# Hybrid decoder block on one core: a weight-sum buffer placed below the head products' pool, ScalarE casts pinned in program order, and an earlier second scan

## The chip, the cores and the metric

The kernel runs on one NeuronCore of one Trainium2 chip. The metric is the device time of one execution in microseconds (us). Five engines work side by side: TensorE (PE: matrix products, with its weight loads listed as PEld), VectorE (DVE), ScalarE (ACT), GpSimd (POOL) and SyncE (SP), which here issues the DMA transfers. Each executes its own instructions strictly in their order and waits, at the head of its queue, for whatever the next instruction needs.

## The reference

One decoder layer on a float32 `x` of 1024 tokens by 1024 channels:

```python
hn = rmsnorm(h, norm_mix); proj = hn @ w_in          # split into 12 parts
y_fox = fox_attention(fq, fk, fv, log_sigmoid(ff + bias))       # 8 heads of 128, causal, with forget bias
q, k, v = split(silu(causal_dwconv([gq, gk, gv], gdn_conv_w)))  # 4 taps
o = gated_delta_rule(l2norm(q), l2norm(k), v, g, beta)          # 8 heads, chunks of 64
y_gdn = rmsnorm(o, gdn_norm) * silu(gz)
h = h + (sigmoid(gate_fox) * (y_fox @ w_branch_fox)
         + sigmoid(gate_gdn) * (y_gdn @ w_branch_gdn)) @ w_out
u = causal_dwconv(rmsnorm(h, norm_ffn) @ w_up)                  # 3 taps
h = h + (silu(u_gate) * u_val) @ w_down
return rmsnorm(h, norm_final)
```

The delta rule is computed in chunks of 64: each needs the inverse of a 64 by 64 unit lower triangular matrix, and then a state of 128 by 128 per head is carried from chunk to chunk.

## The kernel before, in words

**Number format.** A float32 operand is cut into a rounded part (cast on ACT, L106) and the rest (a subtraction on POOL or DVE, L107), and each product is the sum of three: high by high, high by low, low by high. In the profile the pairs are `oh`/`ol` for weights, `yh`/`yl` for activations, `qh`/`ql` and `kh`/`kl` for attention, `vh`/`vl` for its values, `ph`/`pl` for the probabilities. The helper is `split`; `operand` makes an `oh`/`ol` pair, `wsplit` loads a weight tile `wr` and makes two.

**Who sets the order.** PE executes in the order of the code, which is written as generators that are stepped against each other (`take` steps one, `finish` drains it). On DVE, ACT, POOL and SP a scheduler chooses the order of ready work, except where the code pins it: `keep_in_program_order(x)` keeps pinned instructions of one engine in the order of the code, and `issue_after(x)` puts what is issued in its block behind `x` on `x`'s engine. Neither adds a wait on data.

**The stages** in order, with the time each takes in the trace, are in the table below. Those that the change touches:

- *Projection* (`project`): 32 jobs of 84 matmuls (L156, Strassen products of two weight chunks each), operands made three products ahead. Steps taken between matmuls carry other work. First come the delta-rule heads (pool `gin`), in parallel with `prepare_merge`, which adds up branch weights in 16 rounds: a DMA load into a buffer `msum` (L1012, one buffer, inside `gin`), four DVE operations (L993 to L996), a DMA store to `ms` (L1017). When the heads are done, `finish(sums)` drains what is left of those rounds, `gin` is closed, `factors` makes per-token factors (`brk`, and `brk2`, a product with `rk`, L861), and `inverse` starts: it loads `invz` (L940), copies `brk2` twice into `invb2` (L943), lets PE transpose it (L947, L949) and then walks 114 steps of two DVE operations each (L972, L974). Its 135 steps are spread so that they end 420 matmuls before the projection's end. Then `prepare_lead` (first operands of the feed-forward stage) and `fox_first`: loads of the first attention head, `fox_query` and `fox_key` (the casts of `qh` and `kh`), and the first logits (`probs`, L1116 to L1118 on PE).
- *Mix*: the attention of 8 heads (`fox`: per head eight row blocks `probs`, then two halves of `attend`: transposes L1153, products L1144) in 205 steps. Between them, two delta-rule scans are stepped (`stream(0)` for even heads, `stream(1)` for odd): `prep` (loads, POOL scalings of `svt` and `skt` L1241, small products), `scan` (PE L1267, L1272, L1278 to L1281, DVE `sr` and `ss`, ACT `su`, `so`, `sjk`), `columns` (POOL `srs`, `so` L1308; PE transposes L1313; `yge` L1317 on ACT for the last two heads; `ygd` stored). `fox_values` (casts of `vh` on ACT L1072, `vl` on POOL L1073) stands behind row block 5. After the attention both streams are drained.
- *Merge* (`merge`): seven Strassen products per branch (PE L1522), n = 0 to 6, each of four blocks k and 48 matmuls; each block's operands are split on ACT and DVE. After n = 0 of the first branch the columns of the last head are drained (its two `yge`).
- *Output product* (`mix_out`): PE L1514 with `oh`/`ol` of `w_out` and `yh`/`yl` of the merged rows.

Of the kernel before, what the change touches and what calls it, by code (L numbers as in the profile page):

```python
# [17 lines left out]
P = 128  # L18
# [4 lines left out]
H = 8  # L23
# [64 lines left out]
class Block:  # L88
# [14 lines left out]
    def split(self, hi, lo, src, lo_eng=None):  # L103

        nc = self.nc
        nc.scalar.copy(hi, src)  # L106
        (lo_eng or nc.vector).tensor_tensor(lo, src, hi.bitcast(F32), ALU.subtract)  # L107

# [608 lines left out]
    def project(self, blk, fox_pool):  # L717
# [3 lines left out]
        def spill(name, n=H):  # L721
# [10 lines left out]
        rk, self.rq, self.brk, self.brk2, self.kbn = (  # L732
            cp.tile([P, H, NB], F32, name=n) for n in ("rk", "rq", "brk", "brk2", "kbn"))
        gs = ExitStack()
# [122 lines left out]
        def factors():  # L857
# [3 lines left out]
            v.tensor_tensor(self.brk2, self.brk, rk, ALU.mult)  # L861
            v.scalar_tensor_tensor(self.kbn, self.brk2, -1.0, self.egc, op0=ALU.mult, op1=ALU.mult)
# [12 lines left out]
        sums = self.prepare_merge(pool)  # L875
        heads, wait, inv, prep, fox, left = 0, 24, None, None, None, len(jobs) * 84
        with ExitStack() as ix:
            for i, _ in enumerate(self.strassen(jobs, blk, pace=3)):
# [16 lines left out]
                elif inv is None:  # L895
# [3 lines left out]
                    finish(sums)  # L899
# [27 lines left out]
    def inverse(self, ip):  # L927
# [5 lines left out]
        b2 = ip.tile([P, 2, H * NB], F32, name="invb2")  # L933
# [8 lines left out]
        for s in range(2):  # L942
            nc.vector.tensor_copy(b2[:, s], self.brk2.rearrange("p h n -> p (h n)"))  # L943
# [3 lines left out]
        nc.tensor.transpose(ps[:, 0:P], b2.rearrange("p s n -> p (s n)"), self.ident)  # L947
        ps2 = self.small()
        nc.tensor.matmul(ps2[0:Q, 0:Q], self.ident[:, Q:P], b2[:, 0], start=True, stop=True)  # L949
# [70 lines left out]
    def prepare_lead(self, pool):  # L1020
# [5 lines left out]
        def load(src):  # L1026
            t = pool.tile([P, 1024], F32, tag="raw", bufs=4, name="raw")
# [30 lines left out]
    def fox_query(self):  # L1058

        for sl in (slice(0, 512), slice(512, 1024)):  # L1060
            self.split(self.qh[:, sl], self.ql[:, sl], self.ql[:, sl].bitcast(F32), self.nc.gpsimd)

    def fox_key(self):
        for sl in (slice(0, 512), slice(512, 1024)):
            self.split(self.kh[:, sl], self.kl[:, sl], self.kl[:, sl].bitcast(F32), self.nc.gpsimd)
# [881 lines left out]
```

## Time and profile before

| | |
|---|---|
| runs | 2019.66, 2024.9, 2028.93 us; median 2024.9 |
| profiled execution | 2022.93 us, of which the profile's span is 2021.2 us |
| granted TensorE clock, mean of the span | 0.988 |
| busy in the span: ACT, POOL | 1068.1 us (53%), 948.2 us (47%) |

By stage, from a table of windows (us):

| stage | stretch | PE busy | DVE busy | granted clock |
|---|---|---|---|---|
| norm and first operands | 0 to 125 | 108.2 | 85.6 | 1.00 |
| projection, with the heads | 125 to 480 | 336.1 of 355 | 272.1 | 0.98 |
| projection, with the inverse | 480 to 738 | 248.9 of 258 | 237.2 | 0.99 |
| projection, end | 738 to 830 | 90.7 of 92 | 46.9 | 1.00 |
| mix | 830 to 1094 | 242.8 of 264 | 199.1 | 0.97 |
| merge | 1094 to 1260 | 158.0 of 166 | 137.5 | 0.99 |
| output product | 1260 to 1390 | 123.7 of 130 | 88.0 | 0.99 |
| feed-forward, up | 1390 to 1800 | 404.5 of 410 | 302.7 | 1.00 |
| feed-forward, down | 1800 to 2021 | 212.0 of 221 | 126.8 | 0.99 |

"Busy" is the time in which an engine executes something; the rest of a stretch is idle. In a row of the timeline the columns are start, duration, engine, line, operation, output and inputs with their shapes; the bracket, where there is one, is the idle time of that engine just before it and what ended it. "Granted clock" is the TensorE clock that was granted, as a share of full speed; matmuls at 0.50 take twice as long, and count as busy.

### The profile page before, as it was taken

The numbers are of one execution on the slowest core, as the hardware profiler recorded it, in microseconds if no ns is written. First come the engines' busy times: TensorE is split into PE (matmuls) and PEld (weight loads), VectorE is DVE, ScalarE is ACT, GpSimd is POOL, SyncE is SP. The second block draws the span as 40 slices with busy tenths as digits, with TensorE's granted clock in tenths as the row PEclk, the third lists the DMA queues.
The fourth block names the chain that finished last, engine by engine and source line by source line (L and its number), as shares of the span: only waits on it lengthen the run. The fifth ranks groups of instructions, "written<-read, shape, count | busy, mean of one in ns | idle before, by whom it ended". The sixth has DMA issues, their size and how long they took to land. (4 is left out here: it accounts for less than half of the span.)

```text
span 2021.2 us, 29138 instructions
## 1 busy us (share of the span) xinstructions
PE 1924.9 (95%) x9628; PEld 1603.2 (79%) x9628; DVE 1495.9 (74%) x2546; ACT 1068.1 (53%) x2383; POOL 948.2 (47%) x792
## 2 busy tenths in 40 slices
PE   6999999997999899998998999999999999999998
PEld 6988887786878688788987787777788888877886
DVE  7839888864999975477777798577966767777535
ACT  5436777752333355466666444466655555553234
POOL 4735656563545556446563123134666566530012
PEclk9999999998999999899999999999999999999999
DMA  5235555564323277675754853665434343368654
GB/s 193 65 103 165 172 196 177 183 208 162 120 95 109 100 229 265 215 229 200 229 186 160 273 172 109 200 209 174 146 131 136 114 146 126 111 233 330 220 189 162
DMA packets 191608, 350.89 MB, mean 174 GB/s; under 512 B 50784, under 2 KB 79712, under 8 KB 191456
## 3 DMA queue, kind: packets, MB, share of 16 engines
q1 hardware_dynamic: 191312, 348.50, 51.5%
q8 instruction: 76, 1.25, 0.3%
q14 instruction: 76, 0.62, 0.1%
q10 hardware_dynamic: 144, 0.52, 0.1%
HBM read 232.76 MB, written 116.20 MB: 173 GB/s over the span
## 5 line engine op out<-in xcount | busy, mean ns | idle before, releaser
L107 POOL TENSOR_TENSOR ol<-ws,oh 128x512 fp32r<-128x512 f32 x212 | 290.3, 1372 | 232.0 <-ACT oh L106 227.1
L107 POOL TENSOR_TENSOR ol<-wr,oh 128x512 fp32r<-128x512 f32 x165 | 229.0, 1390 | 287.2 <-ACT oh L106 237.6
L106 ACT CAST oh<-ws 128x512 fp32r<-128x512 f32 x212 | 131.0, 618 | 187.3 <-PE mm L156 185.0
L202 DVE TENSOR_TENSOR ws<-wr 128x512 f32<-128x512 f32 x106 | 101.2, 955 | 122.4 <-DMA wr<-in_w_up_dram 65.3
L106 ACT CAST oh<-wr 128x512 fp32r<-128x512 f32 x204 | 123.4, 615 | 120.0 <-PE mm L156 85.5
L382 DVE SCALAR_TENSOR_TENSOR cv<-c,fw,cv 128x512 f32<-128x512 f32 (+2 forms) x176 | 127.5, 748 | 10.9 <-ACT cv L377 9.1
L382 DVE SCALAR_TENSOR_TENSOR cv<-c,cw,cv 128x511 f32<-128x511 f32 (+2 forms) x144 | 105.9, 748 | 8.4 <-ACT cv L377 6.5
L972 DVE TENSOR_TENSOR invt<-invz 128x399 f32<-128x399 f32 (+50 forms) x114 | 96.7, 863 | 0.3
L258 ACT COPY x<-mm 128x512 f32<-128x512 f32 x158 | 92.0, 582 | 5.6 <-PE mm L156 4.5
L156 PE MATMUL mm<-b22h,oh 128*128 128x512 f32 x216 | 85.6, 396 | 6.0 <-ACT x L258 6.0
L156 PE MATMUL mm<-bt1h,oh 128*128 128x512 f32 x216 | 85.3, 395 | 5.9 <-ACT x L258 5.8
L156 PE MATMUL mm<-bt4h,oh 128*128 128x512 f32 x216 | 85.9, 398 | 5.2 <-DVE c L305 5.2
L107 DVE TENSOR_TENSOR ol<-wd,oh 128x512 fp32r<-128x512 f32 x66 | 46.3, 705 | 58.6 <-ACT oh L106 58.6
L156 PE MATMUL mm<-bt4l,oh 128*128 128x512 f32 x216 | 86.9, 402 | 0.0
L156 PE MATMUL mm<-bt2h,oh 128*128 128x512 f32 x216 | 85.3, 395 | 1.3 <-ACT x L258 1.3
L156 PE MATMUL mm<-b21l,oh 128*128 128x512 f32 x216 | 86.2, 399 | 0.0
L156 PE MATMUL mm<-bt2l,oh 128*128 128x512 f32 x216 | 85.8, 397 | 0.3 <-DVE bt2l L107 0.3
L156 PE MATMUL mm<-b22l,oh 128*128 128x512 f32 x216 | 86.0, 398 | 0.0
L156 PE MATMUL mm<-b11h,oh 128*128 128x512 f32 x216 | 84.9, 393 | 1.0 <-ACT oh L106 1.0
L156 PE MATMUL mm<-b11h,ol 128*128 128x512 f32 x216 | 84.8, 393 | 0.6 <-POOL ol L107 0.6
L156 PE MATMUL mm<-bt4h,ol 128*128 128x512 f32 x216 | 85.2, 395 | 0.0
L156 PE MATMUL mm<-b11l,oh 128*128 128x512 f32 x216 | 85.2, 394 | 0.0
(407 smaller groups left out, 6360.8 us busy)
## 6 DMA issues: line engine op xcount, KB each, us to landing
wr<-in_w_up_dram SPq DMA_DIRECT2D x43, 512.0 KB, 3.7
wr<-in_w_gdn_dram SPq DMA_DIRECT2D x24, 512.0 KB, 3.8
wr<-in_w_out_dram SPq DMA_DIRECT2D x24, 512.0 KB, 4.3
s<-hy SPq DMA_DIRECT2D x44, 256.0 KB, 2.8
s<-z SPq DMA_DIRECT2D x44, 256.0 KB, 3.5
wd<-in_w_down_dram SPq DMA_DIRECT2D x44, 256.0 KB, 5.9
b22h<-s SPq DMA_DIRECT2D x44, 256.0 KB, 2.9
b22l<-s SPq DMA_DIRECT2D x44, 256.0 KB, 3.3
```

What stands on the lines that cost most here:

```text
L106: nc.scalar.copy(hi, src)
L107: (lo_eng or nc.vector).tensor_tensor(lo, src, hi.bitcast(F32), ALU.subtract)
L156: self.nc.tensor.matmul(ps, lhs[:, sl], rhs[:, k, :], start=(first and k == 0 and i == 0), stop=(k == 3 and i == 2), skip_group_check=True)
L202: v.tensor_tensor(t, x, y, op)
L258: nc.scalar.copy(t, x)
L382: nc.vector.scalar_tensor_tensor(t[:, lo:], c[:, 512 * j + lo - s:512 * (j + 1) - s], w[:, n - 1 - s:n - s], t[:, lo:], op0=ALU.mult, op1= ...
L972: nc.vector.tensor_tensor(tv, z[:, m:n, 0:n].to_broadcast([P, r, n]), z[:, m, c0:c1].unsqueeze(2).to_broadcast([P, r, n]), ALU.mult))
```

## The change

Line numbers below are those of before unless a row is of the changed kernel.

1. `prepare_merge` gets a pool of its own (`msum`), opened below `gin`, so its rounds need not be drained before `gin` closes: `finish(sums)` moves behind the inverse. `factors` writes `brk2` twice side by side, and PE transposes it directly; the buffer `invb2` and its copies are gone. The step `i % 84 in (24, 64, 80)` that advances the rounds stays.
2. The inverse is spread to end 360 instead of 420 matmuls before the end of the projection; `prepare_lead` has three `raw` buffers instead of four.
3. The casts of `qh` and `kh` (new helper `fox_parts`) are pinned in program order, and `fox_values` comes behind row block 4 instead of 5.
4. The scans: `prep` of head 1 starts at attention step 9 instead of 12, the second stream at 21 instead of 26; stream 0 takes the three steps of its last `columns` inside the stream, so the merge no longer drains them.
5. In the merge, the splits of n = 1 of the first branch stand behind the last `yge`. In the output product, the splits of a weight tile stand behind the `yh` cast before it.

```diff
@@ factors
-            v.tensor_tensor(self.brk2, self.brk, rk, ALU.mult)
-            v.scalar_tensor_tensor(self.kbn, self.brk2, -1.0, self.egc, op0=ALU.mult, op1=ALU.mult)
+            for s in range(2):
+                v.tensor_tensor(self.brk2[:, s], self.brk, rk, ALU.mult)
+            v.scalar_tensor_tensor(self.kbn, self.brk2[:, 0], -1.0, self.egc, op0=ALU.mult, op1=ALU.mult)
@@ project
-        gs = ExitStack()
+        gs, ws = ExitStack(), ExitStack()
+        sums = self.prepare_merge(ws.enter_context(tc.tile_pool(name="msum", bufs=1, reuse_waits="tile")))
         pool = gs.enter_context(tc.tile_pool(name="gin", bufs=1, reuse_waits="tile"))
...
-        sums = self.prepare_merge(pool)
...
-                    finish(sums)
                     gs.close()
                     factors()
...
-                    if (begin - left) * INVERSE_STEPS >= (begin - 420) * steps:
+                    if (begin - left) * INVERSE_STEPS >= (begin - 360) * steps:
                         steps += 1
                         if not take(inv, 1):
                             ix.close()
+                            finish(sums)
...
                     if left % 20 == 0 and not take(prep, 1):
                         ix.close()
+                        ws.close()
                         fox = self.fox_first(fox_pool())
@@ inverse
-        for s in range(2):
-            nc.vector.tensor_copy(b2[:, s], self.brk2.rearrange("p h n -> p (h n)"))
...
-        nc.tensor.transpose(ps[:, 0:P], b2.rearrange("p s n -> p (s n)"), self.ident)
+        nc.tensor.transpose(ps[:, 0:P], self.brk2.rearrange("p s h n -> p (s h n)"), self.ident)
@@ prepare_lead
-            t = pool.tile([P, 1024], F32, tag="raw", bufs=4, name="raw")
+            t = pool.tile([P, 1024], F32, tag="raw", bufs=3, name="raw")
@@ attention
+    def fox_parts(self, hi, lo):
         for sl in (slice(0, 512), slice(512, 1024)):
-            self.split(self.qh[:, sl], self.ql[:, sl], self.ql[:, sl].bitcast(F32), self.nc.gpsimd)
+            raw = lo[:, sl].bitcast(F32)
+
+            self.tc.keep_in_program_order(self.nc.scalar.copy(hi[:, sl], raw))
+            self.nc.gpsimd.tensor_tensor(lo[:, sl], raw, hi[:, sl].bitcast(F32), ALU.subtract)
...
-                if t == 5:
+                if t == 4:
                     self.fox_values()
@@ columns
-                        nc.scalar.activation(y, ps, AF.Copy, scale=self.gn[:, 0:1])
+                        self.evicted = nc.scalar.activation(y, ps, AF.Copy, scale=self.gn[:, 0:1]).ins
@@ mix
+                for _ in range(0 if s else 3):
+                    take(prev, 1)
+                    yield
                 self.last.append(prev)
...
-                if i in (0, 12):
+                if i in (0, 9):
                     preps[i > 0] = prep(int(i > 0))
-                if i in (0, 5, 7):
+                if i in (0, 6, 8):
                     take(preps[0], 1)
-                elif i in (12, 20, 23):
+                elif i in (9, 16, 19):
                     take(preps[1], 1)
-                if i >= 26:
+                if i >= 21:
...
-            for c in self.last:
-                take(c, 1)
+            take(self.last[1], 1)
@@ merge
-            if br == 0:
-                finish(self.last[0])
...
+                    elif br == 0 and n == 1:
+
+                        with self.tc.issue_after(self.evicted):
+                            w, y = self.merge_split(get(wn, k), get(yn, k), v)
@@ mix_out
+                    with self.tc.issue_after(cast) if cast else nullcontext():
+                        w = self.wsplit(a["w_out"][k],
+                                        nc.gpsimd if t0 == 6 and k % 2 == 0 or t0 == 3 and k < 2 else nc.vector)
...
-                            self.split(yh[:, sl], yl[:, sl], src[k][:, zl])
+                            cast = self.split(yh[:, sl], yl[:, sl], src[k][:, zl])
```

What this moves on three engines. First DVE, where `factors` ends and the inverse begins; before:

```order
L995 TENSOR_TENSOR msum<-msum 128x256
L996 TENSOR_TENSOR msum<-msum 128x256
L993 TENSOR_TENSOR msum<-msum 128x256
L994 TENSOR_TENSOR msum<-msum 128x256
L995 TENSOR_TENSOR msum<-msum 128x256
L996 TENSOR_TENSOR msum<-msum 128x256
L943 COPY invb_5134<-brk_1590 128x64 x2
L953 TENSOR_SCALAR invb<-ms 64x64 x2
L950 COPY brh<-ms 64x64
L289 TENSOR_TENSOR c_5175<-mm,x_5090 128x512
```

The same place on DVE with the change:

```order
L864 TENSOR_TENSOR brk_1591<-brk,rk 128x64 x2
L865 SCALAR_TENSOR_TENSOR kbn<-brk_1591,egc 128x64
L866 TENSOR_SCALAR brk<-brk 128x64
L306 TENSOR_TENSOR c_5070<-mm,x_5068 128x512
L993 TENSOR_TENSOR msum<-msum 128x256
L994 TENSOR_TENSOR msum<-msum 128x256
L995 TENSOR_TENSOR msum<-msum 128x256
L996 TENSOR_TENSOR msum<-msum 128x256
L321 TENSOR_TENSOR c_5070<-mm,x_5011 128x512
L203 TENSOR_TENSOR ws<-wr 128x512
```

The tile that PE transposes was the last thing behind the three rounds of sums that follow `factors` (L943; the rows show one and a half of them); now it is written by the second row of `factors` (L864), ahead of all three. One round stays in this place, and L953, which reads the transposed tile, comes six rows behind it; the other two rounds move between the first operations of the inverse, L960.

Second ACT, before the first attention head, where the projection's operands (`oh`), copies of its products (`x`), activations (`c`) and the first exponential (`p`) run; before:

```order
L106 CAST qh<-ql 128x512 x2
L106 CAST oh<-ws 128x512
L760 ACTIVATE c_7917<-c_7917 128x512
L106 CAST kh<-kl 128x512 x2
L106 CAST oh<-wr 128x512
L760 ACTIVATE c_7984<-c_7984 128x512
L106 CAST oh<-ws 128x512
L258 COPY x_8025<-mm 128x512
L106 CAST oh<-wr 128x512 x2
L258 COPY x_8068<-mm 128x512
```

The same stretch of ACT with the change, from the activation `c_7919` (`c_7917` above) on:

```order
L762 ACTIVATE c_7919<-c_7919 128x512
L106 CAST oh<-wr 128x512
L762 ACTIVATE c_7986<-c_7986 128x512
L106 CAST oh<-ws 128x512
L259 COPY x_8027<-mm 128x512
L106 CAST oh<-wr 128x512
L1069 CAST qh<-ql 128x512 x2
L106 CAST oh<-wr 128x512
L259 COPY x_8070<-mm 128x512
L1069 CAST kh<-kl 128x512 x2
```

The casts of `kh` stood ahead of four `oh` casts and two copies of products; now they stand behind all of these, one `oh` cast ahead of the first exponential.

Third POOL in the mix, at the second head's values, where the first scan's `columns` (`srs`, `so`) and the preparation of the next scan (`svt`, `skt`) run too; before:

```order
L1241 TENSOR_TENSOR svt<-svt,brk 128x512 x2
L1306 TENSOR_TENSOR srs<-srs,rq 128x8
L1308 TENSOR_TENSOR so<-so,srs 128x512 x2
L1241 TENSOR_TENSOR skt<-skt,dkl 128x512 x2
L1073 TENSOR_TENSOR vl<-vl,vh 128x512 x2
```

The same place on POOL with the change:

```order
L1246 TENSOR_TENSOR svt<-svt,brk 128x512 x2
L1311 TENSOR_TENSOR srs<-srs,rq 128x8
L1078 TENSOR_TENSOR vl<-vl,vh 128x512 x2
L1313 TENSOR_TENSOR so<-so,srs 128x512 x2
L1246 TENSOR_TENSOR skt<-skt,dkl 128x512 x2
```

`vl` moves ahead of two pairs of POOL operations. On ACT, the merge's rows change as the diff says: with the change all eight casts of n = 1 stand behind the four copies `p` of n = 0 and the two `yge`, where before five of the eight stood ahead of the two `yge`. In the output product the first tile's four `oh` casts stood ahead of all `yh`; with the change the first `yh` stands behind two of them.

More of the change, by code (lines that the diff above doesn't have):

```diff
@@ L1 @@
-from contextlib import ExitStack
+from contextlib import ExitStack, nullcontext
 import numpy as np
@@ L105, in split @@
         nc = self.nc
-        nc.scalar.copy(hi, src)
+        cast = nc.scalar.copy(hi, src)
         (lo_eng or nc.vector).tensor_tensor(lo, src, hi.bitcast(F32), ALU.subtract)
+        return cast.ins
     def operand(self, src, lo_eng=None):
@@ L729, in project @@
         self.gt_d = spill("gtd", 2 * KD)
-        rk, self.rq, self.brk, self.brk2, self.kbn = (
-            cp.tile([P, H, NB], F32, name=n) for n in ("rk", "rq", "brk", "brk2", "kbn"))
-        gs = ExitStack()
+        rk, self.rq, self.brk, self.kbn = (cp.tile([P, H, NB], F32, name=n) for n in ("rk", "rq", "brk", "kbn"))
+        self.brk2 = cp.tile([P, 2, H, NB], F32, name="brk2")
+        gs, ws = ExitStack(), ExitStack()
+        sums = self.prepare_merge(ws.enter_context(tc.tile_pool(name="msum", bufs=1, reuse_waits="tile")))
         pool = gs.enter_context(tc.tile_pool(name="gin", bufs=1, reuse_waits="tile"))
@@ L932, in inverse @@
         br = ip.tile([P, Q], F32, name="invb")
-        b2 = ip.tile([P, 2, H * NB], F32, name="invb2")
         self.y_d = dr.tile([Q, P, Q], F32, name="yd")
@@ L946, in inverse @@
         ps = self.small()
-        nc.tensor.transpose(ps[:, 0:P], b2.rearrange("p s n -> p (s n)"), self.ident)
+        nc.tensor.transpose(ps[:, 0:P], self.brk2.rearrange("p s h n -> p (s h n)"), self.ident)
         ps2 = self.small()
-        nc.tensor.matmul(ps2[0:Q, 0:Q], self.ident[:, Q:P], b2[:, 0], start=True, stop=True)
+        nc.tensor.matmul(ps2[0:Q, 0:Q], self.ident[:, Q:P], self.brk2[:, 0].rearrange("p h n -> p (h n)"), start=True, stop=True)
         nc.vector.tensor_copy(self.brh.rearrange("p h n -> p (h n)"), ps2[0:Q, 0:Q])
@@ L1537, in products @@
             def products(t0, n, ps):
+                cast = None
                 for k in range(KD):
-                    w = self.wsplit(a["w_out"][k], nc.gpsimd if t0 == 6 and k % 2 == 0 or t0 == 3 and k < 2 else nc.vector)
+                    with self.tc.issue_after(cast) if cast else nullcontext():
+                        w = self.wsplit(a["w_out"][k],
+                                        nc.gpsimd if t0 == 6 and k % 2 == 0 or t0 == 3 and k < 2 else nc.vector)
                     yh = pool.tile([P, 3 * P], F32R, tag="yh", bufs=2, name="yh")
```

6 lines of the change are left out of this document (3 added, 3 removed).

## The prediction

> **What bounds the kernel now.** I read the page's first part, then the chain, then PE's timeline for every row with idle time before it, and only then the engine that each such row waited for.
>
> ```profile
> span 2021.2 us, 29138 instructions
> PE 1924.9 (95%) x9628; PEld 1603.2 (79%) x9628; DVE 1495.9 (74%) x2546; ACT 1068.1 (53%) x2383; POOL 948.2 (47%) x792
> ...
> PE 31%; DVE 2%; ACT 1%; POOL 1%; DMA 1%; issue 1%; SPq 0%; POOLq 0%; ACTq 0%; DVEq 0%
> ```
>
> PE works 1924.9 of 2021.2 us, and the chain names it most. The change leaves its products as they are, so there are two things to win: the 96.3 us in which PE idles, and the time in which it works at a lowered clock behind a longer idle. Everything below is counted in these two.
>
> **A. The start of the inverse.** The longest single idle of PE, and what stands before it on DVE and SP (SPq):
>
> ```profile
> 460.96 0.43 DVE L993 TENSOR_TENSOR msum<-msum 128x256 f32<-128x256 f32 x1 [2.87 <-DMA msum<-in_w_branch_dram]
> ...
> 470.32 0.42 DVE L993 TENSOR_TENSOR msum<-msum 128x256 f32<-128x256 f32 x1 [7.08 <-DMA msum<-in_w_branch_dram]
> ...
> 472.04 0.29 DVE L943 COPY invb<-brk 128x64 f32<-128x64 f32 x2
> ```
>
> ```profile
> 446.82 0.23 DVE L861 TENSOR_TENSOR brk<-brk,rk 128x64 f32<-128x64 f32 x1
> ```
>
> ```profile
> 472.47 0.45 PE L947 MATMUL ms<-ident,invb 128*128 128x128 f32 x1 [12.62 <-DVE invb L943]
> ```
>
> ```profile
> 466.07 1.25 SPq L1012 DMA_DIRECT2D msum<-in_w_branch_dram  x2
> ...
> 475.08 2.27 SPq L940 DMA_DIRECT2D invz<-zd  x4
> ```
>
> ```profile
> 472.50:478.00 5.50, 5.50 (x14) 4.20 (x15) 1.35 (x4) 0.00 (x0) 1.29 (x1) 0.51 0.59 175
> ```
>
> The copies that PE's transpose needs stand in DVE's queue behind two rounds that wait 2.87 and 7.08 us for their one buffer: its load (466.07) can only follow the round before. The product that is copied is ready at 447.05. With the change the tile is written there, and the first round behind it no longer holds anything of PE's. PE would want it at 459.85 (472.47 less 12.62), so nothing takes this wait's place: **-12.6 us**. The window behind it (its columns: PE, PE loads, DVE, ACT, POOL busy; granted clock; DMA share; GB/s) shows the clock at 0.51 for 5.5 us, of which half is lost: -2.7 us. The load of `invz`, the last of the SP rows, is issued at the start of the inverse and moves with it. **A is -15.3 us**; the wait alone, -12.6, is its lower bound.
>
> **B. The inverse.** What bounds it, in 25 us windows, and PE's waits in the stage (total, times, longest):
>
> ```profile
> 575.00:600.00 25.00, 22.69 (x92) 18.05 (x92) 24.86 (x40) 7.66 (x14) 9.49 (x8) 0.93 0.29 105
> ...
> 625.00:650.00 25.00, 24.92 (x110) 20.27 (x109) 24.86 (x38) 11.36 (x21) 12.74 (x9) 1.00 0.32 106
> 650.00:675.00 25.00, 20.17 (x83) 15.89 (x82) 24.83 (x36) 7.89 (x15) 10.36 (x7) 0.95 0.24 85
> ```
>
> ```profile
> PE mm L156 <- DVE c L305: 5.2, 2, 2.9
> PE mm L156 <- ACT x L258: 3.8, 2, 1.9
> ```
>
> ```profile
> L972 DVE TENSOR_TENSOR invt<-invz 128x399 f32<-128x399 f32 (+50 forms) x114 | 96.7, 863 | 0.3
> ```
>
> DVE is full here (24.83 to 24.86 of 25), the 114 operations of L972 alone take 96.7 us, and what PE needs of DVE is late by what does not fit: 5.2 + 3.8 = 9.0 us of idle, and by the clocks 0.93 and 0.95 another 1.75 + 1.25 = 3.0 us. The change gives the inverse 60 more matmuls, 60 x 0.227 = 13.6 us (110 of them start in the 24.92 us of the middle window), and puts two rounds of sums into it:
>
> ```profile
> 125.00:480.00 355.00, 45.99 (x64) 0.98 0.56 180
> ```
>
> The row holds DVE's operations on `msum` alone: 64 in 45.99 us make a round of four cost 2.9 us, so 5.7 us are added. Net relief for DVE is 13.6 - 5.7 = 7.9 us against some 12 us of loss. It is not all won: the middle window shows DVE as full with PE hardly idle, so the lateness depends on which steps fall together, not on the mean. Bounds: 0 (they fall together again) and -12. I take **-5 us**, a little under the middle. `prepare_lead` starts 13.6 us later by this; its work lies beside products whose operands are made three products ahead, which cover it, so it is taken at 0; without that cover PE would meet its DVE work as it meets B's.
>
> The bare price of a round is 4 x 0.43 = 1.7 us (by the rows at 460.96 and 470.32). The Trainium skill, "GPSIMD Engine Reference", section 1, says that GpSimd's SBUF interfaces are shared with VectorE and contended by its operations with two SBUF inputs, which these are. In the three windows POOL is busy 9.5 to 12.7 of 25 us, so by that rule the mean of 2.9 holds; by the bare 1.7 the relief would be 2.4 us larger.
>
> **C. The first head's casts.** ACT, POOL and PE before:
>
> ```profile
> 794.26 1.13 ACT L106 CAST kh<-kl 128x512 fp32r<-128x512 f32 x2
> ...
> 804.24 0.58 ACT L258 COPY x<-mm 128x512 f32<-128x512 f32 x1
> ```
>
> ```profile
> 799.46 1.29 POOL L107 TENSOR_TENSOR kl<-kl,kh 128x512 fp32r<-128x512 f32 x1
> ```
>
> ```profile
> 805.61 0.28 PE L1117 MATMUL ms<-kl,qh 128*128 128x256 f32 x1
> ```
>
> Today `kl` is done 4.9 us ahead of L1117. Pinned, the `kh` cast stands behind that copy `x`, which ends at 804.82; half a cast later (0.57) POOL can start, and needs up to 1.3 us for the operand in front and 1.29 us for the first half of `kl`: 806.7 to 808.0, against 805.61. PE's clock may dip behind such a wait, for 0 to 1.75 us by B's first window. Lateness 1.1 to 2.4 and half of that dip make 2.6; **C is +3 us** with the next `oh` cast's `ol` queued behind `kl` on POOL, bounds 0 (the scheduler's queue runs ahead of PE) and +5: a new wait where there is none, L1117 behind POOL's `kl`.
>
> **D. The mix.** PE's waits in 837 to 1095 and the largest of them:
>
> ```profile
> PE us L1267 <- ACT so L1289: 4.0, 3, 1.6
> PE ya L1144 <- POOL vl L1073: 3.9, 2, 3.7
> PE ms L1153 <- DVE p L1132: 2.8, 2, 1.9
> PE ya L1144 <- ACT pf L1161: 1.9, 2, 1.1
> ```
>
> ```profile
> 906.26 2.04 POOL L1241 TENSOR_TENSOR svt<-svt,brk 128x512 f32<-128x512 f32 x2 [2.22 <-DMA svt<-vtd]
> ...
> 908.86 2.04 POOL L1308 TENSOR_TENSOR so<-so,srs 128x512 f32<-128x512 f32 x2
> ...
> 913.24 2.94 POOL L1073 TENSOR_TENSOR vl<-vl,vh 128x512 fp32r<-128x512 f32 x2
> ```
>
> ```profile
> 900.00:925.00 25.00, 20.98 (x153) 18.66 (x152) 18.07 (x61) 16.73 (x51) 18.96 (x20) 0.93 0.64 216
> ```
>
> `vl` moves ahead of `so` and `skt`, so it starts 4.4 us earlier (913.24 - 908.86), at 908.9: the 3.7 us wait goes, with the dip of clock (0.07 x 25 = 1.75 us). It still stands behind `svt` and its 2.22 us of DMA, so nothing more is won there. The `kh` and `qh` casts leave the row blocks for the second half of attention, which should shorten the waits for `so` and `pf`, ACT rows both; but four more casts of ACT then stand among that half's `ph`. And the second scan starts five steps sooner and shares ACT and DVE for longer, with less slack at its end. I count -5.4 for `vl` and -0.6 for the rest: **D is -6 us**, bounds -14 (all four rows and the clock) and +5 (as much again as the new neighbours' waits would cost, by the sum of the third and fourth row).
>
> **E. End of the mix, start of the merge.** The first block after n = 0, and what lies up to n = 2:
>
> ```profile
> 1106.11 1.04 PE L1313 MATMUL ms<-ident,so 128*128 128x128 f32 x8
> ...
> 1111.58 0.50 PE L1522 MATMUL b<-yh,oh 128*128 128x512 f32 x1 [3.04 <-ACT yge L1317]
> ...
> 1119.93 0.50 PE L1522 MATMUL b<-yl,oh 128*128 128x512 f32 x1 [1.20 <-DVE yl L107]
> ...
> 1127.63 0.50 PE L1522 MATMUL a<-yh,ol 128*128 128x512 f32 x1 [2.40 <-DVE ol L107]
> ```
>
> ```profile
> 1110.83 0.69 ACT L1317 ACTIVATE yge<-ms,gn 128x512 f32<-128x512 f32 x1
> ```
>
> ```profile
> 1112.00:1114.00 2.00, 2.00 (x7) 1.27 (x6) 2.00 (x3) 1.03 (x2) 2.00 (x2) 0.70 1.06 384
> ```
>
> n = 1 and its waits take 1127.63 - 1106.11 = 21.5 us, of which 48 x 0.227 = 10.9 are its products, 0.9 the transposes, 6.6 the waits. With the casts behind both `yge` the evictions come first (0.69 us each, the first when half of the transposes are done), then the first pair of casts (1.13, by C's row): ACT is done 0.5 + 1.4 + 1.1 = 3.0 us after 1106.11, and with 0.2 of handing over PE starts 2.3 us after the transposes, where it started at once. If the later waits go, that is 0.9 + 2.3 + 10.9 = 14.1 us, with a dip of clock up to 15.8: a gain of 5.7 to 7.4. Against it: DVE is full (2.00 of 2.00 in the window) and DMA too (1.06), so what DVE must make of n = 1 and of n = 2's sums may be the limit. Bounds -7.4 and +4 (the waits stay, 2.3 and its dip of clock are added). I take **-3.5 us**, with 0.6 of it for the scan's tail, whose steps move into the attention.
>
> **F. Output product.**
>
> ```profile
> PE mm L1514 <- DVE yl L107: 1.8, 1, 1.8
> PE mm L1514 <- ACT yh L106: 0.9, 1, 0.9
> ```
>
> The first `yh` cast moves ahead of two `oh` casts (1.13 us for two casts of that size, by C's row), so the 0.9 goes, and a third of the 1.8 behind it: **-1.5 us**, bounds -2.7 and +2 (the operand casts now pinned behind a `yh` come late once, as the 1.8 did).
>
> **The sum**: -15.3 - 5 + 3 - 6 - 3.5 - 1.5 = -28.3. The profiled execution took 2022.93 us (span 2021.2 and 1.7 around it), so 1994.6; the median of the runs is 2.0 us above it: **1996.6 us**.
>
> On the dips: the windows that hold B's two waits of DVE's `c`, none over 2.9 us, read 0.93 and 0.95. The Trainium skill, "TensorE: Matmul & The Clock Gate", section "Why this matters for your kernels", asks that no idle gap exceed some 3 us. By that rule C's wait would cost no clock, and the sum would be 0.9 us better; these windows speak against it.
>
> **The rivals.** (1) *Only the first wait goes* (chance 0.18): DVE stays full in the inverse, and POOL and ACT in the mix pass the wait on to another row. For it: B's windows and E's, where DVE has no gap; against it the 7.9 us of room in B, and `vl`, which plainly moves. Time: -15.3 + 3 = -12.3, so 2012.6. (2) *The inverse pays it back* (0.06): the rounds come later, each waiting for its buffer on DVE as the 2.87 and 7.08 did, now among operations that PE needs. Two such waits return 9.95 us of the 12.3 that rival 1 leaves: 2022.5, no change. Against it: the rounds' loads are issued 16 matmuls or more ahead by the code. (3) *Slower: handing over from head to head* (0.04). The pinned `kh` cast comes at the fourth step of the second half, so POOL's `kl` may not be there at the next head's L1117.
>
> ```profile
> 921.35 0.66 PE L1153 MATMUL ms<-ident,p 128*128 128x128 f32 x4 [0.18 <-DVE yge L1320]
> ...
> 931.53 0.28 PE L1117 MATMUL ms<-kl,qh 128*128 128x256 f32 x1
> ```
>
> PE takes 10.2 us from that step to L1117; cast and both subtractions need 1.13 + 2.6 = 3.7, so 6.5 us of cover remain, and only `svt` with its DMA (4.3) is seen to stand between. Beyond 6.5 us of lateness each us costs seven heads one us each, so it needs over 5.5 us more in each to eat 28.3 and 10 on top: 2036. (4) *All is won* (0.06): B and D at their better ends, 15 us more than counted, 1981; DVE's full windows speak against it. The forecast has 0.66.
>
> **How the numbers follow.** A difference of 0.5%, 10 us, is about what a measurement of this kernel can tell from no change. Faster by more (below 2014.8): the forecast, (4), and two thirds of (1): 0.84. Within: the rest of (1) and (2): 0.12. Slower: 0.04. The forecast with the spreads of B, D and E reaches from 1984 to 2009; (4) down to 1980 and the better part of (1) up to 2013 leave 0.2 out.
>
> **What would show it.** A: no wait of PE at L947, DVE's `msum` waits behind it. B: fewer than 9 us of idle in 480 to 738, DVE still near full. C: a row L1122 (L1117 before) of about 3 us behind POOL's `kl`. D: no row for `vl` over 1 us; no row for `kl` at later heads. E: one wait of about 2 us behind the `yge`, none of over 1 us behind it. It is wrong if PE's idle falls by less than 10 us, or if a new wait of over 5 us stands in the mix.

## The result, and the profile after

| | before | with the change |
|---|---|---|
| runs | 2019.66 to 2029.95 us, median 2026.67 (5 runs) | 2004.23 to 2011.09 us, median 2005.47 (5 runs) |
| ratio | | 0.9904, 95% interval 0.9879 to 0.9929 |
| span of the profiled execution | 2021.2 us | 2005.4 us |

Faster by 1.0%, 19.5 us by the ratio: the way that was forecast, inside the range, but 9 us less than the 28.3 of the sum. It lies 9 us above the forecast (1996.6) and 7 us below the first rival (2012.6), so the number alone does not choose between them; the terms below do. The page after, first lines:

```profile
span 2005.4 us, 29122 instructions
## 1 busy us (share of the span) xinstructions
PE 1921.8 (96%) x9628; PEld 1602.4 (80%) x9628; DVE 1489.4 (74%) x2545; ACT 1067.3 (53%) x2383; POOL 958.3 (48%) x792
```

PE's idle fell from 96.3 to 83.6 us and its busy time by 3.1: 12.7 + 3.1 are the 15.8 between the spans. To see where, I cut each profile at rows that both kernels have: start of the inverse (L947), first logits (L1116, now L1121), last product of attention, first and third product of the merge, first row of the output product. In the table "idle" is the stretch less PE's busy time, and "clock" is what PE lost to a lowered clock, summed over windows of 2 us as busy time times one less the granted clock.

| stretch (us) | before | idle, clock | after | idle, clock | change once more (e1) |
|---|---|---|---|---|---|
| I to the inverse | 472.5 | 35.8, 0 | 461.8 | 24.4, 0 | 460.2 |
| II to the first logits | 333.0 | 9.7, 5.9 | 328.3 | 9.6, 1.5 | 329.6 |
| III to the end of attention | 285.5 | 21.1, 7.8 | 281.4 | 19.2, 5.4 | 281.4 |
| IV to the merge | 3.6 | | 3.1 | | 3.2 |
| V first two products | 30.0 | 4.5, 1.7 | 34.6 | 5.7, 4.9 | 35.2 |
| VI to the output product | 135.9 | 4.1, 0 | 132.1 | 0.8, 0 | 132.2 |
| VII to the end | 760.7 | 20.4, 1.3 | 763.9 | 21.2, 4.5 | 760.9 |

Stretch V goes from the first row of the first product to the first row of the third, so the transposes of the last head, which stand behind the first product, are in it.

The lines that answer to those of before. The start of the inverse, on DVE, PE and the DMA queue:

```profile
448.48 0.36 DVE L864 TENSOR_TENSOR brk<-brk,rk 128x64 f32<-128x64 f32 x2
```

```profile
461.83 0.27 PE L947 MATMUL ms<-ident,brk 128*128 128x128 f32 x1
```

```profile
450.64 2.06 SPq L942 DMA_DIRECT2D invz<-zd  x4
```

The tile is written 13 us before PE reads it; the PE row has no bracket, so no wait, and `invz` is loaded 24.4 us earlier (475.08 before). The inverse, PE's waits and one window:

```profile
PE mm L157 <- ACT x L259: 5.7, 3, 3.6
PE mm L157 <- DVE c L306: 2.7, 1, 2.7
```

```profile
650.00:675.00 25.00, 22.30 (x97) 18.10 (x98) 24.76 (x37) 8.80 (x17) 10.78 (x8) 1.00 0.30 102
```

8.4 us of waits where there were 9.0, and DVE is as full as before (24.76 of 25). The first head, with the kernel's new wait:

```profile
792.66 0.38 PE L1122 MATMUL ms<-kl,qh 128*128 128x256 f32 x1 [2.21 <-POOL kl L1070]
```

```profile
785.00:800.00 15.00, 12.79 (x53) 10.33 (x52) 4.14 (x14) 7.42 (x17) 10.55 (x10) 0.89 0.25 87
```

2.21 us, and (1 - 0.89) x 15 = 1.7 us of clock. In the mix, the values' rows on POOL:

```profile
893.46 2.48 POOL L1246 TENSOR_TENSOR svt<-svt,brk 128x512 f32<-128x512 f32 x2 [1.91 <-DMA svt<-vtd]
896.07 3.18 POOL L1078 TENSOR_TENSOR vl<-vl,vh 128x512 fp32r<-128x512 f32 x2
899.20 2.50 POOL L1313 TENSOR_TENSOR so<-so,srs 128x512 f32<-128x512 f32 x2
```

`vl` follows `svt` directly, and no row of PE waits for it. The merge is where the change went wrong. First the rows of PE before, at the starts of the first and the third product (the rows between are in the prediction), then PE, ACT, the DMA queue and a window with the change:

```profile
1094.60 0.50 PE L1522 MATMUL a<-yh,oh 128*128 128x512 f32 x1
...
1124.62 0.39 PE L1522 MATMUL a<-yh,oh 128*128 128x512 f32 x1
```

```profile
1074.76 0.50 PE L1531 MATMUL a<-yh,oh 128*128 128x512 f32 x1 [2.76 <-ACT yh L106]
...
1085.07 0.49 PE L1531 MATMUL a<-yh,oh 128*128 128x512 f32 x1 [1.67 <-ACT yh L106]
...
1092.08 1.03 PE L1318 MATMUL ms<-ident,so 128*128 128x128 f32 x8
...
1095.11 0.50 PE L1531 MATMUL b<-yh,oh 128*128 128x512 f32 x1 [2.00 <-ACT yh L106]
...
1097.08 0.79 PE L1531 MATMUL b<-yl,oh 128*128 128x512 f32 x1 [1.47 <-DVE yl L107]
...
1109.34 0.39 PE L1531 MATMUL a<-yh,oh 128*128 128x512 f32 x1
```

```profile
1083.72 0.62 ACT L106 CAST oh<-a 128x512 fp32r<-128x512 f32 x1 [7.98 <-DMA a<-in_w_branch_dram]
```

```profile
1075.97 0.43 SPq L1389 DMA_DIRECT2D a<-in_w_branch_dram  x1
...
1076.99 0.36 SPq L1389 DMA_DIRECT2D a<-in_w_branch_dram  x1
```

```profile
1084.00:1086.00 2.00, 0.70 (x2) 0.39 (x3) 1.63 (x3) 0.96 (x2) 0.00 (x0) 1.00 1.06 404
```

Three things are new. PE waits 2.76 us for the first `yh` of the merge, where eight transposes stood before (stretch IV is no longer for it), and the granted clock is 0.57 from 1076 to 1080 behind it (1.00 there in e1, the same kernel, with the same wait). The first product waits too: ACT sits for 8 us before the cast of its block 3, whose weight (the load at 1076.99) is queued behind ten loads of the second product. Then come the two waits at the second product, whose casts stand behind both `yge`. Behind these two waits the clock dips as well (0.57 from 1086 to 1090, 0.60 from 1096 to 1100).

### The profile page after: what moved, and what is told of

The parts are those of the page before. It is cut to its first block, busy times and chain, and to the rows that moved or that the text cites. A ratio compares the mean times of both kernels' runs of the same rounds, so it can differ in the third digit from the quotient of the medians.

```text
span 2005.4 us, 29122 instructions
## 1 busy us (share of the span) xinstructions
PE 1921.8 (96%) x9628; PEld 1602.4 (80%) x9628; DVE 1489.4 (74%) x2545; ACT 1067.3 (53%) x2383; POOL 958.3 (48%) x792
## 5 line engine op out<-in xcount | busy, mean ns | idle before, releaser
L383 DVE SCALAR_TENSOR_TENSOR cv<-c,fw,cv 128x512 f32<-128x512 f32 (+2 forms) x176 | 127.5, 748 | 10.9 <-ACT cv L378 9.3
L157 PE MATMUL mm<-bt1l,oh 128*128 128x512 f32 x216 | 85.5, 396 | 0.0
```

What stands on the lines that cost most here:

```text
L157: self.nc.tensor.matmul(ps, lhs[:, sl], rhs[:, k, :], start=(first and k == 0 and i == 0), stop=(k == 3 and i == 2), skip_group_check=True)
L383: nc.vector.scalar_tensor_tensor(t[:, lo:], c[:, 512 * j + lo - s:512 * (j + 1) - s], w[:, n - 1 - s:n - s], t[:, lo:], op0=ALU.mult, op1= ...
```

## The experiments

Each ratio is to the kernel before, run on the same chip. "A kernel's stretches" are those of the table.

**e1.** The changed kernel again, no edit.

> The changed kernel once more, unchanged, to see how far its single profile can be trusted. If the stages of its profile are what they are, the marks (start of the inverse, first head, end of the mix, end of the merge, end) come out within 2 us of the first profile of it, and the waits that I read as the change's own are there again: PE for kl at the first head (about 2.2 us), PE for yh in the first product of the merge (about 1.7 us), no wait at the start of the inverse. Rival: that the late idle in the last stage (2.3 us at 1820) and the 1.5 us more idle before the inverse belong to the change; then they are there again, else they are scatter.

2004.27 us, ratio 0.9888 (0.9844 to 0.9932). What I had read as the change's own is there again: 2.19 us for `kl`, 2.88 (for 1.67) in the first product, no wait at L947. Of the rival's two, the wait of 2.29 us at 1820 in the last stretch is there with 1.86 us, but no dip of clock behind it, and the stretch takes 760.9 us for 763.9; the added idle before the inverse is not (22.4 us; 24.4 in the first profile, and 35.8 less the wait of 12.6 before). III, IV, V and VI repeat within 0.6 us here, and III lies between 279.5 and 281.4 in the five profiles whose code is the same up to the merge (after, e1, e4, e5, e6; mean 280.8). I and II vary more: I between 457.8 and 461.8 us in all kernels with this start, II between 327.0 and 329.6 in the eight that share its code up to the pins of e9 (mean 328.3). Differences below such spreads are not read.

**e2.** The kernel before with the first part of the change alone: the pool, `brk2` twice, no copies, the rounds drained behind the inverse; spacing 420.

```diff
+        sums = self.prepare_merge(ws.enter_context(tc.tile_pool(name="msum", bufs=1, reuse_waits="tile")))
...
-        sums = self.prepare_merge(pool)
...
-                    finish(sums)
                     gs.close()
...
                             ix.close()
+                            finish(sums)
```

> The kernel before with only the sums' buffer below the head products' pool (brk2 written twice, no copies, rounds drained behind the inverse), at the old spacing of the inverse (420). Theory: the whole of A comes alone: PE does not wait at the start of the inverse and runs on at full clock, -13 to -15 us against before at that mark, so a ratio of about 0.993; the added rounds make the inverse some 2 to 6 us longer, as DVE is full there. Rival: the inverse gives A back (its rounds wait for their buffer among operations that PE needs): less than -6 us by the first head.

2009.65 us, ratio 0.9912 (0.9878 to 0.9947). No wait at L947; the first logits stand at 790.83, 14.7 us before those of before. So A is real and mostly kept. II is 332.5 us, where before had 333.0 with 2.7 of it the dip behind the wait: the rounds cost about 2.2 us in the inverse, with 11.6 us of idle for 9.7.

**e3.** The changed kernel at the old spacing.

```diff
-                    if (begin - left) * INVERSE_STEPS >= (begin - 360) * steps:
+                    if (begin - left) * INVERSE_STEPS >= (begin - 420) * steps:
```

> The changed kernel with the inverse spread to end 420 matmuls before the projection's end, as before, instead of 360. Theory: the 360 gives little in the inverse and costs the first head: with 420 PE's idle in the inverse rises by 2 to 5 us, but the loads of the first head come some 13 us sooner against PE, its wait for kl (2.2 us and a dip of clock worth 1.7) goes, so the mark of the first head moves by -1 to +2 us. Rival (the prediction): pinning the casts makes the wait for kl, so it stays at about 2.2 us whatever the spacing, and 420 costs 5 us in the inverse: +5 us at the first head's mark.

2004.1 us, ratio 0.9882 (0.9845 to 0.9918), no different from the changed kernel by time. In the profile both sides show. Stretch II takes 334.4 us (mean 328.3 at 360), with 14.2 us of idle:

```profile
PE mm L157 <- ACT x L259: 7.3, 4, 2.5
PE mm L157 <- DVE c L306: 6.7, 4, 2.9
```

And the wait for `kl` is gone, with the casts pinned as they are:

```profile
793.27 0.39 PE L1122 MATMUL ms<-kl,qh 128*128 128x256 f32 x1
```

The prediction's cause for that wait falls here. On ACT the `kh` cast stands ahead of an `oh` cast and a copy `x`, 4.0 us ahead of the first logits (this run); in the changed kernel it stands behind them, 0.8 us ahead:

```profile
789.02 1.14 ACT L1069 CAST kh<-kl 128x512 fp32r<-128x512 f32 x2
...
791.22 0.62 ACT L106 CAST oh<-wr 128x512 fp32r<-128x512 f32 x1 [1.06 <-PE mm L157]
791.74 0.58 ACT L259 COPY x<-mm 128x512 f32<-128x512 f32 x1
```

```profile
788.91 0.58 ACT L259 COPY x<-mm 128x512 f32<-128x512 f32 x1
789.39 1.14 ACT L1069 CAST kh<-kl 128x512 fp32r<-128x512 f32 x2
```

The loads of the first head come behind the inverse and `prepare_lead`; the last rows before the logits are the queue's, first at the old spacing (this run), then in the changed kernel:

```profile
774.58 0.42 SPq L1053 DMA_DIRECT2D ql<-qd  x1
```

```profile
779.43 1.06 SPq L1053 DMA_DIRECT2D ql<-qd  x1
```

That is 18.4 us ahead of the first logits (793.00) at 420, and 10.7 us (790.17) at 360. The mark of the first head moved by +3 us, not by the -1 to +2 that I expected, of which III gave 1 back.

**e4.** The loads of the first branch behind those of block 3.

```diff
                 if (name, k) not in blocks:
-                    blocks[name, k] = self.merge_block(...)
+                    with nullcontext() if br else self.tc.issue_after(self.k3_load):
+                        blocks[name, k] = self.merge_block(...)
```

> The changed kernel with the loads of the first branch's blocks put behind the loads of block 3 of the first product on the DMA issuing queue (in the changed kernel eleven of them stand ahead of it). Theory: the first product of the merge waits for block 3 (its weight lands 8 us after ACT is free for it), so PE's 1.7 us wait there and its dip of clock go, and the first product ends 3 to 5 us sooner; part of it may come back as waits for the second product's blocks, which now land later: -1 to -4 us at the third product. Rival: DMA bandwidth limits the start of the merge (its share is at 1.0), then the order of loads only moves the wait into the second product and the third product starts within 1 us of where it did.

2002.04 us, ratio 0.9875 (0.984 to 0.9909). (Ten loads stood ahead, not eleven.) The first product, counted to the first row of the second and so with the transposes and the wait behind them, takes 16.3 us instead of 20.4, the second 18.3 instead of 14.2: together 34.5, as before the edit. Its wait moved:

```profile
1095.77 0.80 PE L1534 MATMUL b<-yl,oh 128*128 128x512 f32 x1 [5.28 <-DVE yl L107]
```

The time is what the rival said: while the second product's casts are held back, the order of the loads only chooses where PE waits.

**e5.** No order edge in the merge.

```diff
-                    elif br == 0 and n == 1:
-
-                        with self.tc.issue_after(self.evicted):
-                            w, y = self.merge_split(get(wn, k), get(yn, k), v)
```

> The changed kernel without the order edge in the merge (the splits of the second product need not stand behind the last yge). ACT then has most of these casts ahead of the yge, between the copies of the first product. Theory (the edge costs): the wait of 2.0 us at the start of the second product and the 1.5 us behind it go, the wait in the first product (1.7 to 2.9 us, its block 3 lands late) stays, and first and second product together take 31 to 33 us instead of 34.6 and 35.2. Rival (the prediction): the edge saves the later waits of the second product, which come back (3 to 4 us), so the two take 34 to 37 us.

1995.37 us, ratio 0.9837 (0.981 to 0.9865), below the interval of the changed kernel's first measurement (from 0.9879; that of e1 is wider, from 0.9844, and overlaps). V takes 29.2 us (idle 2.2, clock 3.0), where the changed kernel has 34.6 and 35.2, and before had 30.0. No wait of over 1 us comes back behind it:

```profile
1088.72 0.49 PE L1527 MATMUL b<-yh,oh 128*128 128x512 f32 x1 [0.20 <-ACT yge L1322]
...
1094.84 0.50 PE L1527 MATMUL b<-yl,oh 128*128 128x512 f32 x1 [0.78 <-DVE yl L107]
```

On ACT the second product's casts now begin at 1080.55, right behind those of block 3 and 5.5 us ahead of the transposes (1086.09); with the edge they begin at 1093.92, behind the transposes (1092.08).

**e6.** That, and the loads of block 3 ahead of blocks 1 to 3 of the second product (e4's edit with `if br or k == 0`).

> The changed kernel without that edge, and with the loads of block 3 of the first product ahead of those of blocks 1 to 3 of the second on the DMA issuing queue (block 0 stays ahead). Theory (the start of the merge lacks operands, not bandwidth): the first product takes 12 to 15 us instead of 20.4 to 20.9 and the second 14 to 17, together 28 to 31 us, 4 to 7 less than in the changed kernel. Rival (bandwidth: DMA share 1.0 there): together 33 to 35 us, as after the loads of block 3 were put first, with the wait in the second product.

1998.88 us, ratio 0.9853 (0.9824 to 0.9882). First product 14.2 us, second 18.5, together 32.6: between the two expectations, and 3.4 more than without the reordering. Bringing block 3 forward saves its wait and starves the second product for longer.

**e7.** Old starts of the scans (12; 5, 7; 20, 23; 26).

> The changed kernel with the old starts of the scans (steps 12, 5 and 7, 20 and 23, 26). Theory: the earlier second scan is what takes the scan's tail out of the end of the attention, so the stretch from the first head to the end of the mix becomes shorter by the work that leaves it, but the tail behind it grows by 3 us or more, and the merge starts 1 to 4 us later against the first head's mark (281.4 and 3.15 us now, together 284.6). Rival: the second scan's start does not matter (the gain of the mix came from vl and the casts): together within 1 us of 284.6.

2003.88 us, ratio 0.9881 (0.9848 to 0.9914). III and IV together 279.3 + 4.0 = 283.4 us; the changed kernel has 280.8 + 3.1 = 283.9 in the mean. The earlier second scan wins nothing here: the rival. (With the old starts PE waits 1.30 us for the first `yh` of the merge, not 2.76.)

**e8.** Values behind row block 5.

```diff
-                if t == 4:
+                if t == 5:
```

> The changed kernel with the cast of the values behind row block 5 as before. Theory: the wait for vl at the second head (3.7 us before, none now) comes back with its dip of clock, so the stretch from the first head to the end of the mix is 3 to 5.5 us longer than 281.4 us. Rival: with the other casts pinned, vl comes early enough without it: within 1 us of 281.4.

2011.6 us, ratio 0.9922 (0.9895 to 0.9948). III takes 293.5 us, 12.1 more than in the changed kernel, over twice what I expected: some 4.5 of idle and 9 of clock (14.7 for 5.4). The waits for `vl` are back, 3.17 us at 898.35 and 1.04 at 932.13, each with a dip. A wait of 2.31 us for `so` at 1066.93, which the changed kernel doesn't have, brings a third: the granted clock is 0.66 in 895 to 905, 930 to 945 and 1062 to 1072, where the changed kernel has 1.00. By the ratios the difference to the changed kernel is 4 to 7 us, with intervals that overlap.

**e9.** Casts of `qh` and `kh` not pinned.

```diff
-            self.tc.keep_in_program_order(self.nc.scalar.copy(hi[:, sl], raw))
+            self.nc.scalar.copy(hi[:, sl], raw)
```

> The changed kernel without the pin on the casts of qh and kh. Theory: the mix gains by the values' casts one row block sooner, the pins only keep four casts out of the row blocks: the stretch from the first head to the end of the mix grows from 281.4 to 282 to 284 us, waits for so and pf of 1 us or more come back, and the wait for kl at the first head stays at 2.2 us, since its order there does not change without the pin. Rival: the pins carry the mix's gain (285 us or more). Second rival: they cost (under 281).

2006.03 us, ratio 0.9902 (0.9882 to 0.9921). III takes 287.5 us, with 25.1 us of idle for 19.2: the pins do carry 6 us there, as the first rival said (by the times 0 to 2 us: I and VII are shorter in this profile, by scatter as far as I can see). The wait for `kl` at the first head stays as it was without any pin:

```profile
790.49 0.39 PE L1122 MATMUL ms<-kl,qh 128*128 128x256 f32 x1 [2.21 <-POOL kl L1070]
```

**e10.** The first head's steps 20 matmuls later.

```diff
-                elif left < 130 and left % 10 == 0:
+                elif left < 110 and left % 10 == 0:
```

> The changed kernel with the first head's steps taken from 110 instead of 130 matmuls before the projection's end, so that its first logits stand 20 matmuls (4.5 us) later among the products, while its loads come when they did. Theory: PE meets kl 2.2 us too early only because the loads land late, so this wait and its dip of clock go: from the start of the inverse to the end of the mix 606 to 608 us instead of 609.8 to 611.0. Rival: the casts move with the steps and the wait stays, or it moves to the first row blocks behind (over 609).

1998.53 us, ratio 0.9867 (0.9848 to 0.9886). II and III together 603.9 us (607.9 to 611.0 in the five profiles). But the wait for `kl` fell only to 1.48 us, as the casts moved with the steps in part; the rest is idle and clock in III (17.1 and 2.9 for 19.2 and 5.4), whose rows I can't tie to the edit.

**e11.** e5 and e10 together.

> Both at once: no order edge in the merge, and the first head 20 matmuls later. If the two gains are what they seem (5.6 us in the first two products of the merge, 3 to 4 at the first head) and do not meet: 1990 to 1994 us, faster than both kernels. Rival: the earlier end of the mix runs into the loads of the merge, so it stays at 1995 to 1997.

1996.15 us, ratio 0.9852 (0.9835 to 0.9869). V 29.7 us, II and III 606.0: both gains are in the profile, the second smaller, but the time is that of e5 within the intervals. It is also the time of the rival, whose reason shows in small: the wait for block 3 in the first product of the merge is 1.80 us, for 1.02 in e5. Whether the later head adds anything to e5 stays open.

**e12.** e11 with the old starts of the scans.

> The same with the old starts of the scans. Theory: the earlier second scan gains nothing (283.4 us with the old starts against 284.6 up to the merge), so this is within 2 us of the run before it. Rival: with the edge gone the tail of the scan stands in front of the merge again and costs 2 to 4 us.

1998.63 us, ratio 0.9866 (0.9847 to 0.9884): 2.5 us above e11, with intervals that overlap. III and IV are 281.8 us here against 275.8 in e11, where e7 showed no difference. What the scans' starts are worth depends on what stands around them; it isn't settled.

## Why the prediction was right, and where its sum was off

| term | predicted | measured | from |
|---|---|---|---|
| A first wait | -15.3 | -15.3 | no wait at L947, no dip; first logits -14.7 in e2, which has the rounds' 2.2 too |
| B inverse | -5 | -2.0 | II without A's dip: 330.3, now 328.3 (mean) |
| C first head | +3 | +3.9 | 2.2 of wait, 1.7 of clock |
| D mix | -6 | -8.6 | III from 285.5 to 280.8 (mean), with C's 3.9 inside |
| E merge | -3.5 | +1.5 | V +4.9, VI -2.9 without F, IV -0.5 |
| F output product | -1.5 | -0.9 | the wait for `yh` is gone, that for `yl` not |
| sum | -28.3 | -21.4 | the ratio gives -19.5 |

**A** was right in mechanism, place and size. Nothing took the wait's place. In the first profile I fell by 10.7 us only; over the thirteen profiles with the new start it is 459.7 us in the mean, 12.8 less than in the one profile before.

**B** was mis-sized. Its two parts were both there: the rounds cost 2.2 us (e2), and 60 more matmuls gave 4.2 (e2's 332.5 to 328.3) or 6.1 (e3's 334.4). I had set 13.6 us of added room against 5.7 of added work and taken most of the losses for curable. The windows already said otherwise: DVE is as full with the wider spacing (24.76 of 25 us for 24.83), and the waits come where several things of DVE fall together: 2.65 us for a `c` of DVE, and 3.65 us for a copy `x` of ACT, which itself stood behind a wait of 3.79 us for a `c` of DVE.

**C** came out near its size for a wrong reason. The queue that it described is in the trace: the `kh` cast stands right behind a copy `x`, and POOL makes one `ol` before `kl`. The step that failed is the cause, "Pinned, the `kh` cast stands behind that copy `x`". Unpinned at the new spacing the cast stands at the same place and PE waits the same 2.21 us (e9); pinned at the old spacing it stands earlier and PE doesn't wait (e3). So the cause is B's own edit: the inverse and `prepare_lead` end later against PE, and with them the first head's loads, issued 10.7 instead of 18.4 us ahead of their use, and its casts. That it acts through the loads alone is not shown: the `kl` load takes 6.6 us from its issue at 780.55, so it had landed 2.2 us before its cast began, and what held the cast was its place in ACT's queue. I had costed that shift at nothing, as "its work lies beside products whose operands are made three products ahead", and had not followed what is queued behind it. That the wait of 2.21 us also cost 1.7 of clock speaks against the bound of some 3 us that the Trainium skill, "TensorE: Matmul & The Clock Gate", gives in the section that the prediction cites.

**D** was right in its main step: the 3.7 us wait for `vl` and its dip are gone, and e8 brings them back. The pinned casts, which I had given a part of 0.6 us, carry more (6 us of III in e9). The two are not independent: with the pins, undoing the value's step costs 12.1 us of III, more than the 5.4 that its wait cost before: two waits for `vl` and one for `so` then each come with a dip of clock.

**E** had the wrong sign; this is the term that failed. Two steps of it did. The first is what the sum left out: it counts from the transposes on, and puts the first product, ahead of them, at no change. That product went from 11.5 us (1094.60 to 1106.11) to 17.3 (1074.76 to 1092.08), 5.8 more: 2.2 of idle, 1.67 of it for block 3 behind ten loads of the second product, and 3.3 of clock in two dips, one behind that wait and one behind the 2.76 us with which the merge now begins. The second is "If the later waits go, that is 0.9 + 2.3 + 10.9 = 14.1 us". PE did wait 2.00 us behind the transposes, near the 2.3, but a wait of 1.47 us with a dip stayed, and from the transposes to the third product it took 17.3 us (18.5 before). The 21.5 us of the prediction run to the third row of the third product; the like stretch is now 17.7, so 3.8 are won there (the 2.40 in it are gone) and 5.8 lost ahead of it.

e4 shows that the order of the loads alone isn't the loss (34.5 us with block 3 first), e5 that the order edge is: without it V takes 29.2 us, with the loads in the same order, and the transposes and the second product take 13.4 (1086.09 to 1099.49), which is what E had hoped of the edge. ACT waits for block 3 in both; without the edge it then has the second product's casts to do while PE still works on the first product, and with it they begin only after the transposes behind that product. What makes this stretch shorter than before is therefore not the edge; which of the other parts does it, no run isolates. The same holds of the wait of 2.76 us: it is there without the edge too (e5), and e2, which has the first part alone, doesn't have it.

**F**: the 0.9 went, the 1.8 behind it stands unchanged (1.82 at 1244.39).

Of the rivals, the first (only the first wait goes) was right about B and E, where little or nothing was won, and wrong about the mix, which passed no wait on (D). The second (the inverse pays A back) happened in a small way, 2.2 of 15.3 us; the third (lateness at each handover of a head) not at all: no PE row waits for `kl` after the first head. The fourth (all is won) fails at B. The scans' earlier start, of which I had said that it would cost slack, moved III and IV together by half a us on its own (e7).

## What to carry to other kernels

When a row on the chain waits for one late transfer, look which code order or buffer put it there; moving a buffer out of a pool that must be drained was worth most of this change by itself (a ratio of 0.9912, where the whole has 0.9904 and 0.9888). An order edge that holds work behind an event costs whatever that work could have covered before the event, so follow what each engine would have done in the meantime. And when a step is spaced out later, follow what is queued behind it into the next stage: there the price was paid, in a wait that looked like another edit's. A term that a sum leaves out, as E did with the first product, is a forecast of no change and needs a reason too.

## What the runs showed of the hardware that was not expected

A lowered clock doesn't take one long wait. In e8 three short waits of PE, 2.15 us in all within 3.5 us, none over 1.04, came with 9.6 us at half clock, which began before the third of them had ended:

```profile
929.15 0.49 PE L1272 MATMUL us<-ss,skT 128*128 128x128 f32 x2 [0.49 <-ACT so L1294]
...
930.60 0.49 PE L1149 MATMUL ya<-pl,vh 128*128 128x512 f32 x1 [0.62 <-DVE pl L107]
...
932.13 0.80 PE L1149 MATMUL ya<-ph,vl 128*128 128x512 f32 x1 [1.04 <-POOL vl L1078]
```

```profile
931.70:941.30 9.60, 9.16 (x46) 8.73 (x47) 5.12 (x9) 4.00 (x11) 4.81 (x5) 0.50 0.85 330
```

PE works 9.16 of these 9.6 us, so they cost some 4.6 us, more than twice the waits. And the same wait at the same place dips in one execution and not in another: the changed kernel lost 1.5 us to the clock in II, the same kernel in e1 4.7, at nearly the same waits (2.65 and 3.65 us; 2.62 and 3.29). Single profiles of one kernel differ by this much, so terms of 2 us are read from stretches that repeat, not from one span.
